# Low parts on VectorE, grouped activations and a start in program order, in a one-core mLSTM and retention block

## The chip, the cores and the metric

One core of a Trainium2 chip runs the whole block for a batch of one. The metric is the device time of one execution in microseconds (us), the median of several runs. In the profile PE is TensorE (PEld its weight loads), DVE VectorE, ACT ScalarE, POOL GpSimd and SP SyncE, whose queue issues most of the loads.

## The reference

The input has 1024 positions of width 1024; 16 learned meta positions go ahead of them, so the stream has 1040. Everything is float32.

```python
def reference(x, meta_tokens, ...):
    h = concat([meta, x])
    h = h + token_mixer(rmsnorm(h, norm_mix_g), w_in, ...)
    h = h + channel_mixer(rmsnorm(h, norm_ffn_g), ...)
    return rmsnorm(h, norm_final_g)[:, N_META:]

def token_mixer(u, ...):
    proj = u @ w_in                     # q, k, v, o, i, f of 4 mLSTM heads; q, k, v, g of 4 retention heads
    q, k = silu(causal_dwconv(ml_q, ml_k))
    li = 15 * tanh(i / 15); lf = log_sigmoid(f)
    h_ml = sigmoid(ml_o) * head_norm(mlstm_chunkwise(q, k, v, li, lf))
    h_rt = silu(rt_g) * head_norm(retention_chunkwise(rotary(rt_q), rotary(rt_k), rt_v, log_gamma))
    return concat([h_ml, h_rt]) @ w_out

def channel_mixer(u, w_up, w_gate, ffn_conv_w, w_down):
    return (silu(causal_dwconv(u @ w_up)) * (u @ w_gate)) @ w_down
```

The mLSTM weights its scores with exponentials of the gates; the gates need running sums and maxima along the sequence. Inner width of the channel mixer is 2816.

## The kernel before

**Products.** Every large product is made of three matmuls in fp32r: each float32 operand is split into a high part (a cast, on ACT) and a low part (value less high part, a subtraction), and hi·hi, hi·lo and lo·hi are summed in PSUM. In the names, `hi_` and `lo_` are the parts of a weight tile, `raw_` is the tile as loaded, and `u11h`, `u11l` are the parts of the normed stream.

**Stages.** The stream lies in quarters: 11 and 12 are the lower and upper half of the width for the first half of the positions, 21 and 22 those of the second half. Projections to q, k and o go through a scheme with seven products in place of eight (`wino_fm`, `ROWS`); it needs four sums of quarters, S1 to S4, each with a high and a low part. `usum` forms the sums on DVE, and `usplit` splits them: the high part on ACT, the low part on DVE for S1 and S2 and on POOL (`G`) for S3 and S4. The order of the seven products is 11, 12, S2, S1, S3, S4, 22. Their results leave PSUM in `wino_fm`'s evacuations (L826 to L832): copies on ACT (L828, L830) and sums on DVE (L832).

**The first norm** is cut into five ranges of positions, r = 0 to 4. `norm_sums` squares a range (ACT, or half of it on DVE for r < 2), folds the squares on DVE (not for r = 1, which takes eight column sums on PE in place of two), lets PE form column sums (tile `pca`, L688) and takes the root and reciprocal (L690, L691). `norm_split` broadcasts the result on PE (tile `pra`, L700), scales the stream on DVE (L739), casts the high part on ACT (L740) and subtracts for the low part (L744). Between the ranges stand the products for which the range that is ready suffices: `v4_group` (v of head 4 and all gate columns, one chunk of 128 positions, tile `pv`, L800) and `q4_group` (q and k of head 4, tile `pq`, L750 to L752). Then come o, q and k of the heads in the seven-product scheme (tiles `po4x`, `pq0x`, `pq0y`).

**What sets the order.** Each engine runs its instructions in one fixed order. A list scheduler of the framework, which simulates a timeline, makes these orders when the kernel is built: an instruction that is ready by its estimate can go ahead of one that was written earlier. `watch` is called for each instruction as it is written. While `pinned[0]` is true it adds a dependency, without a semaphore, of each PE, DVE and ACT instruction on the one written before it on the same engine; here `pinned[0]` is never true. Once `dealt[0]` is true, side tasks (generators) are advanced between matmul groups by `tick` and `one`, according to a running estimate of each engine's load. `rush` makes them run to their end at once.

**Side tasks that use ACT's function tables**: `sig_tasks` (sigmoid of o for the mLSTM, silu of g for retention, tile `sig`, L871, one task for each half of the width), `tables_tasks` (the mLSTM's decay table `A`: two reads from a scratch in HBM, L955 and L956, a mask, L967 and L968, then nine exponentials with a bias from `cols`, L974), the silu of q and k, the root in the head norm (`z`), and `gates` (tanh, exp, ln, with scans on DVE, tiles `gates`, `gsm`). Between activations of different functions ACT has to load a table (ACT_TABLE_LOAD).

Two copies on POOL (tile `x12`, L1618) and the low parts of S3 and S4 (L1598) are all that POOL does of size in the first 110 us.

Of the kernel before, what the change touches and what calls it, by code (L numbers as in the profile page):

```python
# [65 lines left out]
def body(ctx, tc, h_in, vecs, cst, mask_in, rot, w_v0, w_vp, w_g, w_out, w_up, w_gate, w_down, out):  # L66
# [245 lines left out]
    rush = [False]  # L312

# [37 lines left out]
    def parts(key, pairs, src):  # L351
        for i, (hi, lo) in enumerate(pairs):
            m = AC.copy(hi, src[:, i * HB:(i + 1) * HB])
            if not dealt[0]:
                after(m, last["first"])
# [18 lines left out]
    def need(key, ahead=None):  # L374
# [14 lines left out]
        if mixing[0] and key not in done:  # L389
# [320 lines left out]
    norms = {}  # L710

    def norm_sums(r):
        half, j0, j1 = RNG[r]
        n = j1 - j0
        xs = [xf[f"{half + 1}{i + 1}"][:, :, j0:j1] for i in (0, 1)]
        sq = [x[:, :, j0:j1] for x in sqs]
        AC.activation(sq[0], xs[0], AF.Square)
        if r < 2:
            m = V.tensor_tensor(sq[1], xs[1], xs[1], ALU.mult)
            if r:  # L720
                after(m, last["scale"])
        else:
            AC.activation(sq[1], xs[1], AF.Square)
        if r == 1:
            ss = [x[:, k] for x in sq for k in range(4)]
        else:
            V.tensor_tensor(sq[0], sq[0], sq[1], ALU.add)
            V.tensor_tensor(sq[0][:, 0:2], sq[0][:, 0:2], sq[0][:, 2:4], ALU.add)
            ss = [sq[0][:, k] for k in range(2)]
        norms[r] = xs, rms_sums(ss[0], 0, n, f"a{r}", tmp.tile([P, 5], F32, tag="rcol", name=f"rcola{r}"), "tr", ss[1:])  # L730

    def norm_split(r):
        half, j0, j1 = RNG[r]
        xs, got = norms.pop(r)
        pr = rms_rows(got, None, "upd")
        parts_ = [[u[:, :, j0:j1] for u in UB[f"{half + 1}{i + 1}"]] for i in range(2)]
        for i, x in enumerate(xs):
            for k in range(4):
                last["scale"] = V.scalar_tensor_tensor(x[:, k], x[:, k], vec[:, V_MIX + 4 * i + k:V_MIX + 4 * i + k + 1], pr, ALU.mult, ALU.mult)  # L739
            m = AC.copy(parts_[i][0], x)  # L740
            if r == 0:
                last["first"] = m
        for x, (h_, l_) in zip(xs, parts_):
            last["pace"] = V.tensor_tensor(l_, x, h_.bitcast(F32), ALU.subtract)  # L744
        if r == 0:
            for i, x in enumerate(xs):
                V.tensor_copy(ug[:, 4 * i:4 * i + 4], x[:, :, :32])
# [17 lines left out]
    def v0_split():  # L765
        for i in range(2):
            AC.copy(w0hi[i], w0raw[i])
            G.tensor_tensor(w0lo[i], w0raw[i], w0hi[i].bitcast(F32), ALU.subtract)

# [9 lines left out]
    def v4_group(c, tag, between=None):  # L779
        t0, L = CH[c]  # L780
        nv = 264
        pv = pp(f"pv4_{c}", tag)
        if c == 0:
            for i in range(2):
                for j in range(4):
                    PE.matmul(pv[32 * j:32 * j + 32, :nv], ug[:, 4 * i + j, :], w0raw[i][:, j * nv:(j + 1) * nv],
                                     start=i == 0, stop=i == 1, tile_position=(0, 32 * j))
            t = vz[:META, 264:264 + nv]
            spawn(quads(t, pv, nv))
            V.tensor_copy(gts[:META, :, 0, :], t[:, DV:].rearrange("p (a b) -> p a b", a=2))  # L790
            return
        half = c > 4
        j0 = t0 - 512 * half
        for i, j in ((0, 0), (0, 1), (1, 0)):
# [1525 lines left out]
```

## Time and profile before

| | |
|---|---|
| median of 3 runs | 1550.17 us (1550.03 to 1552.51) |
| the profiled execution | 1552.23 us |
| its span, first to last instruction | 1550.4 us |
| mean granted TensorE clock | 0.987 |
| busy: PE, DVE, ACT, POOL | 97%, 70%, 50%, 5% |

A line of a timeline has the start and the duration in us, engine, line of the program, operation, output and inputs by the program's names, the tile's size, and how many instructions of a kind follow one another; in brackets stands the idle time ahead of it and what ended it. A line of the windows has the stretch, its length, busy time and count for PE, PEld, DVE, ACT and POOL, then the granted clock (1.00 is full speed), the share of time in which the DMA engines were busy, and GB/s; asked for PE alone, it has PE's busy time only. A line of the waits names the waiting instruction, what it waited for, the total in us, the count and the mean. Durations of DVE or ACT groups marked xN cover N instructions.

### The profile page before, as it was taken

How to read it: one execution, taken by the hardware profiler on the slowest of the kernel's cores; microseconds unless marked ns; L12 is line 12 of the kernel's file. 1: busy time of each engine (PE TensorE's matmuls, PEld its weight loads, DVE VectorE, ACT ScalarE, POOL GpSimd, SP SyncE). 2: the span in 40 equal slices, each digit the busy share in tenths (PEclk: the TensorE clock that was granted, in tenths of full speed). 3: DMA queues.
4: the chain of work that ended last, by engine and by line, in shares of the span. 5: the costliest groups of instructions: out<-in, count | busy, mean ns of one | idle time of the engine just before them, and what ended most of it. 6: DMA issues, size and time to landing. Idle time of an engine off the chain costs nothing.

```text
span 1550.4 us, 25495 instructions
## 1 busy us (share of the span) xinstructions
PE 1503.9 (97%) x9929; PEld 1361.5 (88%) x9929; DVE 1080.2 (70%) x2103; ACT 772.2 (50%) x1467; POOL 83.8 (5%) x137
## 2 busy tenths in 40 slices
PE   7988999999999999999999999999999999999997
PEld 6978998899889999997888988999999999888887
DVE  7695867676677567755768778667666666778657
ACT  5365647574665345644355455444444444434443
POOL 1030000000000000000000001222220000000000
PEclk8999999999999999999999999999999999999999
DMA  6021345333632355589333327887873223933213
GB/s 228 1 82 56 109 132 179 99 98 122 206 95 90 109 170 177 188 308 334 121 106 119 103 80 229 209 211 190 196 190 89 82 82 121 385 113 108 100 45 109
DMA packets 104586, 223.81 MB, mean 144 GB/s; under 512 B 10520, under 2 KB 33760, under 8 KB 104288
## 3 DMA queue, kind: packets, MB, share of 16 engines
q1 hardware_dynamic: 95872, 199.02, 38.6%
q0 software_dynamic: 8448, 23.07, 7.5%
q8 instruction: 78, 1.28, 0.3%
q14 instruction: 44, 0.36, 0.1%
q10 hardware_dynamic: 144, 0.07, 0.0%
HBM read 178.05 MB, written 67.15 MB: 158 GB/s over the span
## 4 chain that ended last, share of the span: by engine, by line
PE 85%; DMA 7%; DVE 4%; ACT 3%; issue 1%; SPq 0%; DVEq 0%; ACTq 0%
PE pdx L762 3%; PE pdx L761 3%; PE pdx L760 3%; PE pup_x L761 2%; PE pup_x L762 2%; PE pup_x L760 2%; PE pga_x L760 2%; PE pga_x L761 2%; PE pga_x L762 2%; PE pdy L762 2%; PE pdy L761 2%; PE pdy L760 2%; PE pv L800 2%; PE pwx L762 2%; PE pwx L760 2%; PE pwx L761 2%
## 5 line engine op out<-in xcount | busy, mean ns | idle before, releaser
L644 ACT CAST hi_up<-raw_up 128x512 fp32r<-128x512 f32 (+1 forms) x52 | 36.4, 719 | 107.3 <-PE pga_z L761 61.1
L760 PE MATMUL pup_x<-uh_g,hi_up 128*128 128x256 f32 (+1 forms) x240 | 67.4, 283 | 1.2 <-ACT uh_g L1731 1.2
L645 DVE TENSOR_TENSOR lo_ga<-fraw_ga,hi_ga 128x512 fp32r<-128x512 f32 (+1 forms) x52 | 41.8, 807 | 37.3 <-ACT hi_ga L644 37.1
L645 DVE TENSOR_TENSOR lo_up<-raw_up,hi_up 128x512 fp32r<-128x512 f32 (+1 forms) x52 | 41.3, 809 | 37.9 <-ACT hi_up L644 37.0
L761 PE MATMUL pup_x<-ul_g,hi_up 128*128 128x256 f32 (+1 forms) x240 | 67.5, 283 | 0.1
L762 PE MATMUL pup_x<-uh_g,lo_up 128*128 128x256 f32 (+1 forms) x240 | 66.5, 283 | 0.0
L645 DVE TENSOR_TENSOR lo_d<-rd,hi_d 128x1024 fp32r<-128x1024 f32 (+1 forms) x34 | 37.6, 1112 | 32.8 <-ACT hi_d L644 32.7
L644 ACT CAST hi_ga<-fraw_ga 128x512 fp32r<-128x512 f32 (+1 forms) x52 | 36.4, 719 | 45.1 <-PE pup_z L761 24.0
L762 PE MATMUL pdx<-uh_d,lo_d 128*128 128x512 f32 (+1 forms) x156 | 57.9, 375 | 0.0
L761 PE MATMUL pdx<-ul_d,hi_d 128*128 128x512 f32 (+1 forms) x156 | 57.8, 374 | 0.0
L644 ACT CAST hi_d<-rd 128x1024 fp32r<-128x1024 f32 (+1 forms) x34 | 32.3, 959 | 49.3 <-PE pdy L761 32.5
L762 PE MATMUL pdy<-uh_d,lo_d 128*128 128x512 f32 x132 | 51.9, 393 | 0.0
L761 PE MATMUL pdy<-ul_d,hi_d 128*128 128x512 f32 x132 | 51.7, 392 | 0.0
L760 PE MATMUL pdx<-uh_d,hi_d 128*128 128x512 f32 (+1 forms) x156 | 48.5, 372 | 0.0
L760 PE MATMUL pdy<-uh_d,hi_d 128*128 128x512 f32 x132 | 47.9, 389 | 0.0
L760 PE MATMUL pga_x<-uh_g,hi_ga 128*128 128x512 f32 x120 | 47.5, 396 | 0.0
L761 PE MATMUL pga_x<-ul_g,hi_ga 128*128 128x512 f32 x120 | 47.5, 396 | 0.0
L760 PEld LDWEIGHTS pup_x<-uh_g,hi_up 128*128 128x128 f32 x240 | 45.4, 190 | 2.3 <-ACT uh_g L1731 1.4
L762 PE MATMUL pga_x<-uh_g,lo_ga 128*128 128x512 f32 x120 | 47.1, 393 | 0.0
L761 PEld LDWEIGHTS pup_x<-ul_g,hi_up 128*128 128x128 f32 x240 | 45.5, 190 | 1.0 <-DVE ul_g L1732 0.3
L762 PEld LDWEIGHTS pup_x<-uh_g,lo_up 128*128 128x128 f32 x240 | 44.8, 189 | 0.8
L526 POOL DMA_DIRECT2D wsd<-w_down_d x33 | 19.9, 748 | 467.1 <-DVE s2up L1959 466.6
(1685 smaller groups left out, 5814.4 us busy)
## 6 DMA issues: line engine op xcount, KB each, us to landing
raw_up<-w_up_d SPq DMA_DIRECT2D x22, 512.0 KB, 4.3
fraw_ga<-w_gate_d SPq DMA_DIRECT2D x22, 512.0 KB, 4.2
acts<-cv SPq DMA_DIRECT2D x44, 256.0 KB, 4.3
wsd<-w_down_d POOLq DMA_DIRECT2D x44, 256.0 KB, 6.6
rd<-wsd SPq DMA_DIRECT2D x22, 512.0 KB, 3.6
raw_w<-w_out_d SPq DMA_DIRECT2D x20, 512.0 KB, 4.2
wsw<-raw_w SPq DMA_DIRECT2D x32, 256.0 KB, 3.2
raw_m<-w_out_d SPq DMA_DIRECT2D x14, 512.0 KB, 4.9
```

Of the source, the lines that this page charges most:

```text
L526: dep(G.dma_start(x, y), last["pace"], True)
L644: AC.copy(hi[:, o:o + n], x)
L645: V.tensor_tensor(lo[:, o:o + n], x, hi[:, o:o + n].bitcast(F32), ALU.subtract)
L760: m.append(PE.matmul(pt, ah, xh_, start=first and k == 0, stop=False, skip_group_check=True))
L761: PE.matmul(pt, ah, xl_, start=False, stop=False, skip_group_check=True)
L762: m.append(PE.matmul(pt, al, xh_, start=False, stop=last and k == n - 1, skip_group_check=True))
L800: PE.matmul(pv[:, :nv], u[:, kb % 4, j0:j0 + L], (w0hi, w0lo)[j][kb // 4][:, o:o + nv], start=i + j + kb == 0, stop=i == 1 and kb == KB - ...
```

## The change

The edit has three parts.

1. The low parts of S3 and S4 are subtracted on DVE (`V`), as those of S1 and S2 are.
2. Side tasks that use a function table take turns. `table_turn(who)` lets a task go on when no other one holds the turn; `table_free()` gives it back. Both halves of `sig` are now one task, and so are the nine exponentials of `A`. `gates` doesn't ask for the turn.
3. The start is written out as one sequence, with `pinned[0]` true from the first square to the low part of range 4. Groups of matmuls are cut finer (`v4` takes one of the three products and some of the contraction blocks), `q4_group` runs its three products one after another rather than side by side, all five ranges fold their squares, and range 1 squares on ACT alone. The cast of the second half of head 4's v weights (`w0hi[1]`) is written after the root of range 0. The splits of q's weights are held in `hold` and ended at a chosen place. Chunks 5 to 8 and the rest stand behind the pinned part.

```diff
@@ -283,10 +283,15 @@
     evacs = []
     dealt = [False]
 
+    hold = []
+
     def spawn(g, q=pend):
         if dealt[0]:
             if next(g, pend) is not pend:
                 q.append(g)
+        elif hold:
+            next(g)
+            hold.append(g)
         else:
             for _ in g:
                 pass
@@ -310,6 +315,16 @@
                     q.remove(g)
 
     rush = [False]
+    turn = [None]
+
+    def table_turn(who):
+        while dealt[0] and not rush[0] and turn[0] not in (None, who):
+            yield
+        turn[0] = who
...
+    def table_free():
+        turn[0] = None
...
@@ -351,7 +366,7 @@
     def parts(key, pairs, src):
         for i, (hi, lo) in enumerate(pairs):
             m = AC.copy(hi, src[:, i * HB:(i + 1) * HB])
-            if not dealt[0]:
+            if not dealt[0] and not pinned[0]:
                 after(m, last["first"])
         yield
         for i, (hi, lo) in enumerate(pairs):
...
         issue(i + 1 + ahead)
-        if mixing[0] and key not in done:
+        if mixing[0] and not hold and key not in done:
             forced.append(key)
             rush[0] = True
             while key not in done:
...
-
-    def norm_sums(r):
+    def xr(r, i):
...
+    def square(r, i, vector=False):
+        if vector:
+            V.tensor_tensor(sqr(r, i), xr(r, i), xr(r, i), ALU.mult)
...
-    def norm_split(r):
+            AC.activation(sqr(r, i), xr(r, i), AF.Square)
+
+    def fold(r):
+        a, b = sqr(r, 0), sqr(r, 1)
+        V.tensor_tensor(a, a, b, ALU.add)
+        V.tensor_tensor(a[:, 0:2], a[:, 0:2], a[:, 2:4], ALU.add)
+
+    def sums_(r):
+        a = sqr(r, 0)
+        return rms_sums(a[:, 0], 0, a.shape[2], f"a{r}", tmp.tile([P, 5], F32, tag="rcol", name=f"rcola{r}"), "tr", [a[:, 1]])
...
+    def ur(r, i, j):
         half, j0, j1 = RNG[r]
...
+        return UB[f"{half + 1}{i + 1}"][j][:, :, j0:j1]
+
+    def scale(r, i, pr):
+        x = xr(r, i)
+        for k in range(4):
+            V.scalar_tensor_tensor(x[:, k], x[:, k], vec[:, V_MIX + 4 * i + k:V_MIX + 4 * i + k + 1], pr, ALU.mult, ALU.mult)
+        last["first"] = AC.copy(ur(r, i, 0), x)
+
+    def low(r, i):
+        last["pace"] = V.tensor_tensor(ur(r, i, 1), xr(r, i), ur(r, i, 0).bitcast(F32), ALU.subtract)
 
...
-    def v4_group(c, tag, between=None):
...
+
+    def v4_first():
+        nv = 264
...
+        yield
+        yield from quads(t, pv, nv)
...
+        yield
+
+    def v4(c, i, j, kbs=range(KB)):
...
+        if c not in bank4:
+            bank4[c] = pp(f"pv4_{c}", next(ring0))
...
+        for kb in kbs:
...
+            PE.matmul(bank4[c][:, :nv], u[:, kb % 4, j0:j0 + L], (w0hi, w0lo)[j][kb // 4][:, o:o + nv], start=i + j + kb == 0, stop=i == 1 and kb == KB - 1, skip_group_check=True)
+
+    def v4_out(c):
+        pv = bank4[c]
+        AC.copy(vtile[4][c > 4][:, (c - 1) % 4 * VW:(c - 1) % 4 * VW + DV], pv[:, :DV])
...
+
+    def q4_group(i, half, j0, j1):
+        w = ready["q4", i]
+        pt = pp(f"pq4{i}{half}{j0}", next(ring0))[:, :j1 - j0]
+        for n, (a, b) in enumerate(((0, 0), (1, 0), (0, 1))):
             for kb in range(KB):
...
-    def q4_group(i, half, j0, j1, tag):
...
+                PE.matmul(pt, w[kb // 4][b][:, kb % 4 * P:(kb % 4 + 1) * P], UB[f"{half + 1}{kb // 4 + 1}"][a][:, kb % 4, j0:j1], start=n + kb == 0, stop=n == 2 and kb == KB - 1, skip_group_check=True)
+            yield
         AC.copy(raws[i][:, half * 512 + j0:half * 512 + j1], pt)
+        yield
...
@@ -866,11 +881,16 @@
...
     def sig_tasks(h):
-        def f(b):
+        def f():
             yield from lag(1.5)
-            AC.activation(sigt[:, b], sigt[:, b], AF.Sigmoid if h < H else AF.Silu)
-            done.add(("sig", h, b))
-        return [(lambda b=b: f(b), 0, None) for b in range(2)]
+            yield from table_turn(("sig", h))
+            for b in range(2):
+                AC.activation(sigt[:, b], sigt[:, b], AF.Sigmoid if h < H else AF.Silu)
+                done.add(("sig", h, b))
+                if b == 0:
+                    yield
+            table_free()
+        return [(f, 0, None)]
 
...
@@ -967,11 +987,15 @@
...
+            yield
+            yield from table_turn(("tab", h))
             for x in (range(5), range(5, NCH)):
-                yield
...
                     AC.activation(A1[:, t0:t0 + L], A1[:, t0:t0 + L], AF.Exp, bias=cols[:, 0, c * H + h:c * H + h + 1])
+                if x[0] == 0:
+                    yield
+            table_free()
             done.add(("tab", h))
         return [(make, 0, None)]
 
@@ -1002,9 +1026,11 @@
...
+            yield from table_turn(("qk", h))
             for i in range(2):
                 d = qk[i][1]
                 AC.activation(d[:, a:b], d[:, a:b], AF.Silu)
+            table_free()
             done.add(("qk", h, r))
 
...
@@ -1436,9 +1462,12 @@
...
                 yield
+                yield from table_turn(("z", h))
                 AC.activation(z[:, :n], z[:, :n], AF.Sqrt)
             else:
+                yield from table_turn(("z", h))
                 AC.activation(z[:, :n], mv[:, 0:n, 1], AF.Sqrt, bias=cs[:, C_EPS + h - H:C_EPS + h - H + 1])
+            table_free()
             yield
...
@@ -1557,26 +1586,102 @@
...
-    norm_sums(0)
-    v0_split()
-    norm_split(0)
-    v4_group(1, next(ring0), lambda: norm_sums(1))
-    need(("q4", 0), 1)
-    norm_split(1)
-    v4_group(0, next(ring0))
-    v4_group(2, next(ring0))
-    norm_sums(2)
-    q4_group(0, 0, 0, 272, next(ring0))
-    norm_split(2)
-    q4_group(1, 0, 0, 272, next(ring0))
-    norm_sums(3)
-    for c in (3, 4):
-        v4_group(c, next(ring0))
-    norm_split(3)
-    norm_sums(4)
+    def end(g):
+        for _ in g:
+            pass
+
+    def v4_all(c):
+        for i, j in ((0, 0), (0, 1), (1, 0)):
+            v4(c, i, j)
+
+    lower, upper = range(4), range(4, KB)
+    pinned[0] = True
+    square(0, 0)
+    square(0, 1, True)
+    fold(0)
+    AC.copy(w0hi[0], w0raw[0])
+    pr = rms_rows(sums_(0), None, "upd")
     for i in range(2):
-        q4_group(i, 0, 272, SB, next(ring0))
-    norm_split(4)
+        if i:
+            AC.copy(w0hi[i], w0raw[i])
+        G.tensor_tensor(w0lo[i], w0raw[i], w0hi[i].bitcast(F32), ALU.subtract)
+    square(1, 0)
+    scale(0, 0, pr)
+    square(1, 1)
+    scale(0, 1, pr)
+    v4(1, 0, 0)
+    fold(1)
+    v4(1, 0, 1, lower)
+    got = sums_(1)
+    low(0, 0)
+    v4(1, 0, 1, upper)
+    v4(1, 1, 0, lower)
+    low(0, 1)
+    v4(1, 1, 0, upper)
+    pr = rms_rows(got, None, "upd")
+    hold.append(None)
+    need(("q4", 0), 0)
+    for i in range(2):
+        V.tensor_copy(ug[:, 4 * i:4 * i + 4], xr(0, i)[:, :, :32])
+    scale(1, 0, pr)
+    v4_out(1)
+    scale(1, 1, pr)
+    meta = v4_first()
+    next(meta)
+    need(("q4", 1), 0)
+    v4(2, 0, 0)
+    v4(2, 0, 1)
+    low(1, 0)
+    low(1, 1)
+    v4(2, 1, 0)
+    end(hold[1])
+    square(2, 0)
+    square(2, 1)
+    fold(2)
+    end(hold[2])
+    hold.clear()
+    end(meta)
+    q = q4_group(0, 0, 0, 272)
+    next(q)
+    next(q)
+    got = sums_(2)
+    v4_out(2)
+    next(q)
+    pr = rms_rows(got, None, "upd")
+    scale(2, 0, pr)
+    end(q)
+    scale(2, 1, pr)
+    q = q4_group(1, 0, 0, 272)
+    for _ in range(3):
+        next(q)
+    square(3, 0)
+    square(3, 1)
+    end(q)
+    low(2, 0)
+    low(2, 1)
+    fold(3)
+    v4_all(3)
+    v4_out(3)
+    got = sums_(3)
+    v4_all(4)
+    pr = rms_rows(got, None, "upd")
+    scale(3, 0, pr)
+    scale(3, 1, pr)
+    v4_out(4)
+    square(4, 0)
+    square(4, 1)
+    end(q4_group(0, 0, 272, SB))
+    low(3, 0)
+    low(3, 1)
+    fold(4)
+    got = sums_(4)
+    end(q4_group(1, 0, 272, SB))
+    pr = rms_rows(got, None, "upd")
+    scale(4, 0, pr)
+    scale(4, 1, pr)
+    low(4, 0)
+    low(4, 1)
+    pinned[0] = False
...
@@ -1595,7 +1700,7 @@
...
             AC.copy(h_, part(x, i))
-            (G if nm in ("S3", "S4") else V).tensor_tensor(l_, part(x, i), h_.bitcast(F32), ALU.subtract)
+            V.tensor_tensor(l_, part(x, i), h_.bitcast(F32), ALU.subtract)
 
...
@@ -1605,13 +1710,15 @@
...
     for c in (5, 6):
-        v4_group(c, next(ring0))
+        v4_all(c)
+        v4_out(c)
     for i in range(2):
-        q4_group(i, 1, 16, 272, next(ring0))
+        end(q4_group(i, 1, 16, 272))
     for c in (7, 8):
-        v4_group(c, next(ring0))
+        v4_all(c)
+        v4_out(c)
     for i in range(2):
-        q4_group(i, 1, 272, SB, next(ring0))
+        end(q4_group(i, 1, 272, SB))
     usplit("S3", "21", "r2", "r3")
```

Three places of the new order, each before and after.

PE around the column sums of the last range (`pca_529` before, `pca_551` now). Before:

```order
L700 MATMUL pra_508<-cs,rcola_444 128x16
L700 MATMUL pra_508<-cs,rcola_444 128x128 x2
L688 MATMUL pca_529<-cs,sqr_132 128x1 x4
L750 MATMUL pq_536<-u11h,hi_q_0_0_289 128x256
L751 MATMUL pq_536<-u11l,hi_q_0_0_289 128x256
```

Now, from the q products (`pq_681`) that stand ahead of them:

```order
L822 MATMUL pq_681<-u22h,hi_q_0_0_283 128x256
L822 MATMUL pq_681<-u21l,hi_q_0_0_283 128x256 x4
L822 MATMUL pq_681<-u22l,hi_q_0_0_283 128x256 x4
L703 MATMUL pca_551<-cs,sqr_132 128x1 x4
L822 MATMUL pq_558<-u11h,hi_q_1_0_310 128x256 x4
```

The sums moved from behind the broadcast of range 3 to behind chunks 5 and 6 and most of a q group of the second half of the positions, none of which is in the pinned part.

ACT from the last copy of head 4's gate to head 0's first q evacuation (`rawq<-pq0x`). Before:

```order
L828 COPY sig<-po4x_895 128x256
L353 CAST hi_q_3_0_1180<-raw_q0b 128x512
L353 CAST hi_q_3_0_1180<-raw_q0a 128x512
L871 ACT_TABLE_LOAD
L871 ACTIVATE sig<-sig 128x1026 x2
L353 CAST hi_q_5_0_1283<-raw_q0b 128x512
L353 CAST hi_q_5_0_1283<-raw_q0a 128x512
L1109 ACT_TABLE_LOAD
```

Now:

```order
L843 COPY sig<-po4x_891 128x256
L888 ACT_TABLE_LOAD
L888 ACTIVATE sig<-sig 128x1026
L1120 ACT_TABLE_LOAD
L1120 ACTIVATE gsm<-gsm 1x36
L1042 COPY rawq<-rawk 64x528
L1043 COPY rawq<-rawk 64x528
L368 CAST hi_q_3_0_1176<-raw_q0b 128x512
L368 CAST hi_q_3_0_1176<-raw_q0a 128x512
L1042 COPY rawq<-rawk 64x512
L1043 COPY rawq<-rawk 64x512
L888 ACT_TABLE_LOAD
```

The two halves of the gate's silu were neighbours with one load; now the exponential of the gates (`gsm`), four copies of the rotary and two casts stand between them: the exponential has a load of its own, and the second half has to load its table again.

ACT at head 0's decay table (`A_0`). Before:

```order
L830 ACTIVATE rawk<-pq0x_1234 128x264
L353 CAST hi_vp_0_0_1431<-raw_vp_11_1308 128x512 x2
L830 ACTIVATE rawk<-pq0x_1257 128x264
L974 ACTIVATE A_0_1642<-A_0_1642,cols 128x16
L974 ACTIVATE A_0_1642<-A_0_1642,cols 128x128 x2
```

Now:

```order
L845 ACTIVATE rawk<-pq0x_1230 128x264
L995 ACTIVATE A_0_1638<-A_0_1638,cols 128x16
L995 ACTIVATE A_0_1638<-A_0_1638,cols 128x128 x8
L368 CAST hi_vp_0_0_1437<-raw_vp_11_1304 128x512 x2
L845 ACTIVATE rawk<-pq0x_1253 128x264
```

All nine exponentials and the two casts moved ahead of the second evacuation of `pq0x`. In the whole order there are 46 table loads now, 44 before.

More of the change, by code (lines that the diff above doesn't have):

```diff
@@ L732, in norm_split @@
-    def norm_split(r):
-        half, j0, j1 = RNG[r]
[L734 to L747, printed above, removed]
+        return xf[f"{half + 1}{i + 1}"][:, :, j0:j1]
@@ L763, in mm3s @@
         return m[0], m[-1]
[L765 to L768, printed above, removed]
     def quads(dst, pv, n):
@@ new lines, in body @@
+    square(1, 0)
[14 more added lines that the diff above has]
+    need(("q4", 0), 0)
+    for i in range(2):
+        V.tensor_copy(ug[:, 4 * i:4 * i + 4], xr(0, i)[:, :, :32])
[3 more added lines that the diff above has]
+    meta = v4_first()
```

52 lines of the change are left out of this document (12 added, 40 removed).

## The prediction

> **What bounds the kernel now.** I read the page first, then the PE windows, then the timelines of the first 135 us, because the order of instructions differs only in short stretches.
>
> ```profile
> PE 1503.9 (97%) x9929; PEld 1361.5 (88%) x9929; DVE 1080.2 (70%) x2103; ACT 772.2 (50%) x1467; POOL 83.8 (5%) x137
> PE 85%; DMA 7%; DVE 4%; ACT 3%; issue 1%; SPq 0%; DVEq 0%; ACTq 0%
> 0.00:80.00 80.00, 69.19 (x487) 66.91 (x488) 56.64 (x111) 37.63 (x60) 8.12 (x10) 0.94 0.32 111
> 80.00:120.00 40.00, 30.51 (x229) 28.27 (x227) 34.74 (x69) 24.25 (x42) 11.63 (x5) 0.91 0.25 80
> 120.00:600.00 480.00, 469.47 (x3622) 439.93 (x3623) 327.62 (x774) 270.03 (x547) 8.46 (x44) 0.99 0.41 127
> ```
>
> TensorE (PE) is the bound; its idle time is 46.5 us of the span, 20.3 us of it before 120 us (10.8 and 9.5). So a gain can only come from there, or from a clock that is granted earlier. How fast PE runs depends on that clock:
>
> ```profile
> 34.04 1.08 PE L800 MATMUL pv<-w0hiq,u11l 128*128 128x264 f32 x4
> 34.92 1.08 PE L800 MATMUL pv<-w0hik,u12l 128*128 128x264 f32 x4
> 41.74 0.65 PE L800 MATMUL pv<-w0hiq,u11h 128*128 128x264 f32 x4
> 42.23 0.65 PE L800 MATMUL pv<-w0hik,u12h 128*128 128x264 f32 x4
> 34.00:36.00 2.00, 2.00 (x11) 0.50 0.00 0
> 100.00:102.00 2.00, 0.25 (x2) 0.75 0.61 173
> 106.00:108.00 2.00, 2.00 (x12) 0.55 0.00 0
> ```
>
> Four matmuls take 0.88 us at a clock of 0.50 and 0.49 us at 1.00, so 0.22 and 0.122 each (0.126 for 272 columns and 0.1185 for 256, by the same spacing). The dip at 101 us lasts about 6.8 us and costs half of that; it begins at the end of a PE wait.
>
> **The start, to the last matmul of the norm stage.** In the new order the square root of the first norm goes ahead of the cast of w0hik, and the second norm adds its squares on VectorE (DVE), so its column sums are 2 float32 matmuls and not 8.
>
> ```profile
> 8.87 1.07 ACT L767 CAST w0hik<-w0raw 128x1056 fp32r<-128x1056 f32 x1 [0.28 <-DMA w0raw<-w_v_d]
> 9.85 0.26 ACT L690 ACTIVATE rcola<-pca,vec 128x2 f32<-128x2 f32 x1
> 11.37 1.71 PE L688 MATMUL pca<-cs,sqr 128*128 128x1 f32 x8
> 13.56 1.25 PE L800 MATMUL pv<-w0hiq,u11h 128*128 128x264 f32 x4 [0.49 <-ACT u11h L740]
> ```
>
> The first large matmul moves from 13.56 to 12.7 (0.85 for the cast). Six float32 matmuls at two records of 0.22 each are 2.7 us less. Followed through with the durations above, pv of chunk 2 ends at 28.4; before, it ended at 35.6 (34.92 and four matmuls). That is 7.2 us, but not all of it is kept. Before, PE had by then done column sums of ranges 2 and 3 as well; now these are still ahead. From 28.4 there are 48 matmuls of 0.126 (6.05), 144 of 0.122 (17.6), 144 of 0.1185 (17.1), 4.9 of norm matmuls and 0.4 at half clock: 46.0. To this come waits which program order makes, because range 3's norm follows range 2's with little between: 1.05 for u12h, 1.4 for the folded squares, 1.2 for u22h. Sum 28.4 + 46.0 + 3.7 = 78.1, against 78.3 before. I take nothing for the start. Bounds: 2.5 better, if the clock rises one stretch earlier (24 matmuls at 0.122), 2 worse, if a wait lets it fall.
>
> **The last norm comes late.** At the first place shown in the section on the change, the column sums of range 4 (pca) followed the broadcast of range 3 (pra) at once. The sums now stand behind chunks 5 and 6 and most of a q group, which are not pinned and were hoisted.
>
> ```profile
> 55.43 3.22 DVE L739 SCALAR_TENSOR_TENSOR x<-x,vec,pra 128x256 f32<-128x256 f32 x8 [1.16 <-PE pra L700]
> 71.50 1.25 DVE L1598 TENSOR_TENSOR uS2l<-x,uS2h 128x1056 fp32r<-128x1056 f32 x1
> 91.87 0.38 PE L760 MATMUL po4x<-uS2h,hi_o 128*128 128x256 f32 x1 [2.49 <-ACT sig L828]
> ```
>
> DVE's scaling starts at 63.1 instead of 55.43 (PE reaches the sums at 58.7, then 24 matmuls, then the broadcast). Behind it DVE has 25.6 us without a pause up to the low part of S2, which ends at 88.7 and not at 72.7. PE needs it at 86.7: new waits of about 2.0, then 2.3 for S1's high part and the evacuations. They replace waits of 3.5 us (2.49, 0.78, 0.22) there. Price so far +0.8.
>
> **Low parts of S3 and S4 on DVE.** What GpSimd (POOL) does to DVE:
>
> ```profile
> 80.38 5.77 POOL L1598 TENSOR_TENSOR uS3l<-x,uS3h 128x1056 fp32r<-128x1056 f32 x2
> 81.23 5.47 DVE L358 TENSOR_TENSOR lo_o<-raw_o4b,hi_o 128x512 fp32r<-128x512 f32 x2 [0.27 <-ACT hi_o L353]
> 101.95 1.28 DVE L358 TENSOR_TENSOR lo_q<-raw_q0a,hi_q 128x512 fp32r<-128x512 f32 x2
> 95.28 5.48 POOL L1598 TENSOR_TENSOR uS4l<-s,uS4h 128x1056 fp32r<-128x1056 f32 x2 [9.13 <-ACT uS4h L1597]
> 94.98 0.38 DVE L1071 TENSOR_TENSOR_SCAN gates<-gates 36x128 f32<-36x128 f32 x1
> 98.42 2.62 DVE L1073 TENSOR_TENSOR_SCAN gates<-gates 36x128 f32<-36x128 f32 x1
> PE pe L1079 <- DVE gsm L1075: 3.0, 1, 3.0
> ```
>
> Beside POOL, two DVE splits took 5.47 instead of 1.28 and a scan 2.62 instead of 0.38; with one more gate step that is 8.6 us. The four moved parts add 4 x 1.17 = 4.7 (L1598 at 1.25, less overlap). DVE is 3.9 us ahead, the scan is no longer held, PE's 3.0 us wait goes and the dip at 101 us with it. The two copies on POOL (L1618) stay. Carried through, PE ends the matmuls of po4x with u22 at 104.7 instead of 109.7: 5.0 ahead.
>
> **Grouped activations give it back.** Counted in the two orders, table loads rise from 44 to 46. At the second place shown, ACT between the last copy of o4 and q0's first evacuation, one half of head 4's output gate (tile sig) went ahead of the gates' exponential (gsm), so the other half, further down, needs a load of its own.
>
> ```profile
> L871 ACT ACT_TABLE_LOAD x11 | 14.1, 1283 | 0.2
> 109.95 0.35 ACT L828 COPY sig<-po4x 128x256 f32<-128x256 f32 x1
> 112.89 2.01 ACT L871 ACTIVATE sig<-sig 128x1026 f32<-128x1026 f32 x2
> 119.96 0.63 ACT L828 COPY rawq<-pq0x 128x264 f32<-128x264 f32 x2
> 120.37 0.39 PE L760 MATMUL pq0x<-uS2h,hi_q 128*128 128x264 f32 x1 [3.38 <-ACT rawq L828]
> ```
>
> From the copy at 104.9, ACT has three loads before the last one, four in all (5.1), the two halves of sig (2.0), four rotary copies (2.5, L1042 and L1043, which ran earlier before), four casts (2.1), the gates' small steps and copies (1.8): 13.5, so 118.4 against 120.37. PE, which arrives at 112.4, waits 6.0 instead of 3.4 us. Of 5.0 ahead 2.0 are left.
>
> Next, the third place, head 0's table A. The evacuation of pq0x's second chunk, for which PE waits before S3, now stands behind all nine exponentials and two casts, and those wait for a transfer through HBM.
>
> ```profile
> 0.00:24.00 24.00, 15.02 (x74) 12.83 (x74) 12.78 (x33) 13.34 (x21) 5.18 (x8) 1.00 0.98 341
> ...
> 120.49 0.35 SPq L955 DMA_DIRECT2D A<-scr  x1
> 121.37 2.27 SPq L956 DMA_DIRECT2D A<-scr  x2
> 124.33 0.18 DVE L967 TENSOR_TENSOR A<-A,mask 128x16 f32<-128x16 f32 x1 [3.21 <-DMA A<-scr]
> 126.49 0.38 ACT L830 ACTIVATE rawk<-pq0x 128x264 f32<-128x264 f32 x1
> 127.54 1.22 DVE L968 TENSOR_TENSOR A<-A,mask 128x1024 f32<-128x1024 f32 x1 [3.03 <-DMA A<-scr]
> 130.09 1.85 ACT L974 ACTIVATE A<-A,cols 128x128 f32<-128x128 f32 x6
> 131.95 0.29 PE L760 MATMUL pq0y<-uS4h,hi_q 128*128 128x264 f32 x1
> 135.73 0.49 PE L1353 MATMUL s<-qT,kT 128*128 128x128 f32 x2 [0.97 <-DVE pt L1377]
> ```
>
> The read of A is issued at about 119.6 (1.8 earlier), with two weight tiles (raw_vp, 512 KB each) ahead of it in place of one. Before, from the first issue at 121.37 the second piece took some 6 us to the mask add at 127.54; one more weight tile takes 1.5 at the 341 GB/s of the window of the first 24 us (DMA busy share 0.98); so it lands near 127.2; mask 1.2, cols 0.2, nine exponentials 2.6, two casts 1.1, the evacuation 0.3: PE goes on at 132.6. Before, it started that group at 130.5 (131.95 less 12 matmuls). So 2.1 late; PE is there at 128.7 and waits 3.9. The later wait of 0.97 for DVE is covered now, which makes +1.1.
>
> A wait of this length ends in a dip. The dips of the trace cost 3.4 (6.8 us) and 1.7 (that at 121 us); the one at 121 us has its counterpart after the wait of 6.0, the second wait adds one. I take the mean, 2.5. All the rest I cost at nothing: the second extra load lies near 315 us under PE at 100%, and if ACT has no slack there it costs 1.3; from about 665 us on the orders agree.
>
> The Trainium skill (TensorE: Matmul & The Clock Gate, section "Why this matters for your kernels") states that gaps above about 3 us between bursts take the clock down. The trace agrees for the wait of 3.0 ahead of 101 us. By the page's busy window of about 3.4 us a dip would cost an estimated 1.7, and the sum would be 0.8 lower.
>
> **Sum.** 0 (start) + 0.8 - 5.8 = -5.0 at 104.7; +3.0 on ACT; +4.1 at A's exponentials; -1.0; +2.5 clock: **+3.6 us**. The profiled execution has a span of 1550.4 and took 1552.23, so it would be 1555.8; the median of the runs, 1550.17, lies 2.06 below that execution, which gives **1553.8**.
>
> **Rivals.** *The exponentials don't hold PE* (faster). If A lands in 3.8 us, as its first piece did (issued 120.49, used 124.33), ACT is through by 128.8 and PE hardly waits: -2.0, -1.0, and no second dip; from a landing before 123.5 on this decides. 1547. For it: the transfer itself is small; against: two weight tiles are ahead.
>
> *The hold without the dip* (no change): +1.1, 1551.3. A wait of 2.49 at 89 us left the clock at 1.00; against it: 3.0 and 3.4 did not.
>
> *Dips everywhere* (slower): the broken stretch at 86 to 92 us and a wait in the start each cost a dip too: +3.6 + 2 x 2, 1558. For it: PE is busy there about a third of the time; against: from 87 to 92 it was hardly busier before, at 1.00.
>
> **How the numbers follow.** Forecast 0.42, faster rival 0.22, no change 0.20, dips 0.16. A measurement of this kernel tells about 0.2%, 3.1 us, from no change; the forecast lies just above it, and I split it 0.27 slower, 0.13 no change, 0.02 faster. The faster rival lies at the bound too: 0.19 faster, 0.03 no change. Of the no-change case 0.13 stay there, 0.06 are slower, 0.01 faster. With the dips that makes faster 0.22, no change 0.29, slower 0.49. Range 1546 to 1561: downward the faster rival with another 1 of the start's 2.5; upward the dips with the start's 2 and the 1.3 at 315 us. The forecast's own range is 1551.5 to 1556.5.
>
> **What would show it.** Right: scaling of range 4 starts near 63; PE waits near 88 for uS2l, near 112 to 118 for rawq, and some 4 us at S3 of q0 for rawk behind the exponentials; the clock at 0.50 after both; no DVE split above 2 us but beside POOL's copies. Wrong: PE without a wait from 125 to 135, or ahead by 3 us or more at 140, or behind already at 78.

## The result and the profile after

The changed kernel takes 1564.04 us (median of 4 runs, 1560.94 to 1566.96), the kernel before beside it 1551.32. The ratio is 1.0084, 95% interval [1.0067, 1.0102]: slower by 12.7 us, where 3.6 were forecast. The profiled execution took 1564.91 us with a span of 1562.2, 11.8 more than before.

The page of the changed kernel (busy time of each engine) and its windows, with the columns of those before:

```profile
PE 1503.5 (96%) x9917; PEld 1359.8 (87%) x9917; DVE 1079.2 (69%) x2108; ACT 774.3 (50%) x1470; POOL 75.0 (5%) x133
0.00:80.00 80.00, 62.33 (x447) 58.63 (x448) 46.56 (x101) 29.78 (x51) 5.19 (x8) 0.94 0.37 124
80.00:120.00 40.00, 34.03 (x257) 31.86 (x256) 36.83 (x73) 28.59 (x46) 3.56 (x2) 0.96 0.18 54
120.00:600.00 480.00, 461.01 (x3519) 431.31 (x3520) 321.67 (x762) 266.69 (x535) 10.66 (x44) 0.98 0.39 123
```

PE's busy time is the same to 0.4 us (1503.9 before). So the whole 11.8 us are idle time of PE: 6.9 more before 80 us (17.7 against 10.8), 3.5 less from 80 to 120 (6.0 against 9.5), 8.5 more from 120 to 600 (19.0 against 10.5).

The waits in the start, from PE's timeline:

```profile
12.66 1.25 PE L810 MATMUL pv<-w0hiq,u11h 128*128 128x264 f32 x4 [1.99 <-ACT u11h L755]
21.28 0.76 PE L810 MATMUL pv<-w0hiq,u11h 128*128 128x264 f32 x4 [0.83 <-ACT u11h L755]
23.43 1.25 PE L810 MATMUL pv<-w0hik,u12h 128*128 128x264 f32 x4 [1.39 <-ACT u12h L755]
36.92 0.75 PE L810 MATMUL pv<-w0hiq,u11h 128*128 128x264 f32 x4 [1.90 <-ACT u11h L755]
42.68 1.81 PE L703 MATMUL pca<-cs,sqr 128*128 128x1 f32 x12 [1.49 <-DVE gts L815]
55.52 0.75 PE L810 MATMUL pv<-w0hik,u22h 128*128 128x264 f32 x4 [0.88 <-ACT u22h L755]
```

At ranges 0 to 3 PE waits for the cast that follows the scaling; the row at 42.68 is the exception, column sums that wait for DVE, where a copy of the gates stands behind the folded squares. The last matmul of the stage ends at 83.6 us; it was 78.4 before. DVE behind it:

```profile
67.23 3.22 DVE L754 SCALAR_TENSOR_TENSOR x<-x,vec,pra 128x256 f32<-128x256 f32 x8 [2.92 <-PE pra L715]
86.70 1.24 DVE L1703 TENSOR_TENSOR uS2l<-x,uS2h 128x1056 fp32r<-128x1056 f32 x1
89.68 2.41 DVE L1703 TENSOR_TENSOR uS3l<-x,uS3h 128x1056 fp32r<-128x1056 f32 x2
92.02 1.24 DVE L1703 TENSOR_TENSOR uS2l<-x,uS2h 128x1056 fp32r<-128x1056 f32 x1
96.42 2.34 DVE L1703 TENSOR_TENSOR uS1l<-s,uS1h 128x1056 fp32r<-128x1056 f32 x2
```

Range 4 is scaled from 67.2 (55.43 before), and from there DVE has no pause up to 99 us. It was idle 2.9 us just ahead, waiting for PE. The second half of S2's low part is through at 93.3 (72.7 before), and for it PE waits 1.0 us. ACT, PE and DVE at the gates:

```profile
111.69 0.37 ACT L843 COPY sig<-po4x 128x256 f32<-128x256 f32 x1 [2.23 <-PE po4x L773]
112.08 1.28 ACT L888 ACT_TABLE_LOAD   x1
113.37 1.06 ACT L888 ACTIVATE sig<-sig 128x1026 f32<-128x1026 f32 x1
114.45 1.28 ACT L1120 ACT_TABLE_LOAD   x1
119.74 1.28 ACT L888 ACT_TABLE_LOAD   x1
123.14 1.28 ACT L1135 ACT_TABLE_LOAD   x1
125.23 0.66 ACT L843 COPY rawq<-pq0x 128x264 f32<-128x264 f32 x2
135.88 2.64 ACT L995 ACTIVATE A<-A,cols 128x16 f32<-128x16 f32 x9 [6.50 <-DVE cols L1143]
...
125.62 0.40 PE L1142 MATMUL pt<-cs,gates 36*128 36x36 f32 x2 [5.82 <-DVE gates L1138]
135.90 0.61 PE L1379 MATMUL s<-qT,kT 128*128 128x16 f32 x2 [3.08 <-DVE cols L1143]
...
130.37 0.18 DVE L987 TENSOR_TENSOR A<-A,mask 128x16 f32<-128x16 f32 x1 [3.62 <-DMA A<-scr]
133.13 1.22 DVE L446 TENSOR_TENSOR raw_vp<-raw_vp,raw_vp 128x1024 f32<-128x1024 f32 x1 [2.58 <-DMA raw_vp<-w_vp_d]
134.44 1.22 DVE L988 TENSOR_TENSOR A<-A,mask 128x1024 f32<-128x1024 f32 x1
135.58 0.26 DVE L1143 COPY cols<-pt 128x108 f32<-128x108 f32 x1
```

Four loads between 112 and 124.4, and PE waits 5.8 us until it can transpose the gates, which come out of these exponentials. Another wait of 3.1 us follows at 133 to 136: PE's score matmul `s` needs the copied columns (`cols`), and on DVE these stand behind a sum of weights (`raw_vp`), which waits 2.6 us for its load, and behind the second part of the mask of `A`.

### The profile page after: what moved, and what is told of

It reads as the page before. It is cut to its first block, busy times and chain, and to the rows that moved or that the text cites. A ratio compares the mean times of both kernels' runs of the same rounds, so it can differ in the third digit from the quotient of the medians.

```text
span 1562.2 us, 25485 instructions
## 1 busy us (share of the span) xinstructions
PE 1503.5 (96%) x9917; PEld 1359.8 (87%) x9917; DVE 1079.2 (69%) x2108; ACT 774.3 (50%) x1470; POOL 75.0 (5%) x133
## 4 chain that ended last, share of the span: by engine, by line
PE 83%; DVE 7%; DMA 6%; ACT 3%; issue 1%; SPq 0%; DVEq 0%; ACTq 0%
PE pdx L773 3%; PE pdx L772 3%; PE pdx L771 3%; PE pup_x L772 2%; PE pup_x L773 2%; PE pga_x L771 2%; PE pup_x L771 2%; PE pga_x L772 2%; PE pga_x L773 2%; PE pdy L773 2%; PE pdy L772 2%; PE pdy L771 2%; PE pwx L773 2%; PE pwx L771 2%; PE pwx L772 2%; PE n L1429 2%
## 5 line engine op out<-in xcount | busy, mean ns | idle before, releaser
L772 PE MATMUL pdx<-ul_d,hi_d 128*128 128x512 f32 (+1 forms) x156 | 57.8, 374 | 0.0
L659 ACT CAST hi_d<-rd 128x1024 fp32r<-128x1024 f32 (+1 forms) x34 | 32.3, 959 | 48.8 <-PE pdy L772 32.5
```

Of the source, the lines that this page charges most:

```text
L659: AC.copy(hi[:, o:o + n], x)
L772: PE.matmul(pt, ah, xl_, start=False, stop=False, skip_group_check=True)
```

## The experiments

All times are medians beside runs of the kernel before on the same chip; the ratio is to those. Chips differ by a microsecond or two, so kernels of different sets are compared by their ratios (0.001 is 1.55 us). An idle time or a place in a timeline is that of the one execution that was profiled, which lies up to 5 us from its kernel's median.

**The three parts apart.** Each kernel has one or two of them. Undoing or doing a part is, for the low parts and the turns:

```diff
-            (G if nm in ("S3", "S4") else V).tensor_tensor(l_, part(x, i), h_.bitcast(F32), ALU.subtract)
+            V.tensor_tensor(l_, part(x, i), h_.bitcast(F32), ALU.subtract)
```

```diff
+            yield from table_turn(("sig", h))
...
+            table_free()
```

together with the one task for both halves in `sig_tasks` and for all exponentials in `tables_tasks`. The start is that of one kernel or the other.

Low parts alone.

> The kernel before with one edit: the low parts of S3 and S4 on DVE. Theory A (my prediction's second step): without POOL beside it DVE is no longer held up, PE's wait of 3.0 us at 98 us and the half-clock stretch behind it go, so the last product of head 4's gate ends about 5 us earlier (104 in place of 109.2) and the whole is 3 to 5 us faster, near 1547. Rival: DVE is 4.7 us busier just where PE waits for it, so the gain is eaten at once and the time stays within 2 us of 1551.

Turns alone.

> The kernel before with one edit: side tasks that use a function table take turns. Theory A: the turns cost PE waits by themselves, at head 0's q (3 to 7 us before its S3 products) and at head 2's q (3.5 us near 300 to 345 us): 1556 to 1561. Rival B (the start alone is to blame, and whatever follows is only late with it): within 2 us of 1551.

Start alone.

> The changed kernel with the other two edits undone, so that of the change only the start in program order is left. Theory A: 5.2 us late at the first product of head 4's gate (83.5 in place of 78.2), and little after it: 1554 to 1557. Rival B: the same 5.2 us there, and most of the later loss with it: 1560 to 1564.

Low parts and turns with the old start.

> The kernel before with the low parts on DVE and the turns, but its own start. Theory A: 5 us gained at head 4's gate and 5 to 8 lost behind it: 1551 to 1556. Rival B: 1546 to 1550, the low parts' gain and no loss.

The change without the turns.

> The changed kernel without the turns; the start in program order and the low parts on DVE stay. Theory A: PE's waits for the gates (5.8 us at 120 us) and for the copied columns behind A (3.1 us at 133 us), and those near 290 to 345 us, shrink by 4 us together: 1558 to 1561. Rival (the waits come from the late start alone): 1563 to 1565.

The change with the low parts back on POOL.

> The changed kernel with the low parts of S3 and S4 back on POOL. If they are worth nothing at the end: 1562 to 1566, as the changed kernel. If a busier DVE is what hurts behind a late norm: 3 us or more faster; if DVE beside POOL is slower still: 3 us or more slower.

| parts in the kernel | us | ratio [95%] |
|---|---|---|
| low parts | 1549.88 | 0.9995 [0.9981, 1.0009] |
| turns | 1552.71 | 1.0013 [0.9995, 1.0031] |
| low parts, turns | 1554.74 | 1.0030 [1.0014, 1.0045] |
| start | 1560.49 | 1.0060 [1.0039, 1.0082] |
| start, low parts | 1561.16 | 1.0061 [1.0040, 1.0082] |
| start, turns | 1562.35 | 1.0073 [1.0045, 1.0101] |
| all three | 1564.04 | 1.0084 [1.0067, 1.0102] |

By the ratios of the pairs of rows that differ in one part, the start costs 8.4 to 10.2 us, the turns 2.0 to 5.4, the low parts between -0.8 and +2.6; the intervals of the rows are 2 to 4 us to either side, so only the start's cost is certain in each pair. The rival "the start alone is to blame" is nearer than my theory, which had put most of the loss on the turns. With the low parts alone the gain that I had forecast is there at 120 us and gone at 200: in the windows of PE (second figure of a row: busy time), idle from 80 to 165 us falls from 10.8 to 2.7, and 9.5 us come back at 165 to 200, where head 4's norm holds PE. Before, low parts alone:

```profile
80.00:165.00 85.00, 74.17 (x538) 0.94 0.25 75
```

```profile
80.00:165.00 85.00, 82.29 (x642) 1.00 0.30 94
...
PE tr L1458 <- ACT v4lo L1449: 4.7, 1, 4.7
PE tr L1458 <- DVE mx L1466: 2.3, 1, 2.3
```

The last two rows are PE's waits from 165 to 200 us. PE had run ahead with products of the next head and then had nothing to put beside head 4's chain.

In the kernel with start and low parts but without the turns, ACT has the same order behind the start, four loads between the same activations, and PE the same wait of 5.8 us for the gates; its wait for `cols` is 1.7 us there and not 3.1. So most of what I had called the turns' doing isn't theirs. What is theirs lies later: the wait for `rawk` and for the merge (`mx`) near 320 to 340 us is there with them and not without, first the changed kernel from 285 to 350 us, then the one without turns:

```profile
PE tr L1487 <- DVE mx L1495: 1.6, 1, 1.6
PE pq2x L771 <- DVE rawk L847: 1.6, 2, 1.2
```

```profile
PE s L1358 <- DVE pt L1377: 0.8, 1, 0.8
```

**What in the start costs it.** First without program order, the flag staying false:

```diff
-    pinned[0] = True
+    pinned[0] = False
```

> The changed kernel with the start's instructions free again (the flag stays false there), its code as it is. Theory S1 (program order itself makes PE wait): PE's idle time in the first 60 us falls from 17.7 to about 11 us, head 4's gate begins near 78 in place of 83.5, and the whole comes to that of the two other edits alone, 1553 to 1557. Theory S2 (what was rewritten in the start makes the waits: folded squares of range 1, q's three products one after another, held splits): idle stays at 16 us or more, 1561 to 1566.

Measured 1556.20, ratio 1.0039 [1.0022, 1.0056]. That is 7.0 us below the changed kernel, though PE's idle time in the first 60 us is 15.2, between the numbers of the two theories: from 80 to 165 us 2.1 us are idle and not 14.7, and at 165 to 200 us 9.8 come back, as with the low parts alone. So the order costs some 7 us, and the waits in the start, 2.5 us shorter, are not where most of them go.

Then program order on DVE and ACT only:

```diff
-        if pinned[0] and nm in before:
+        if pinned[0] and nm != "PE" and nm in before:
```

> The changed kernel with only PE free of the program order in the start; DVE and ACT keep it. If PE's own order makes the waits (products that are ready stand behind ones that are not): idle of the first 60 us falls to 11 to 13 us, 1553 to 1558. If it is the order on DVE and ACT (the norms come late, whatever PE does meanwhile): idle stays at 16 us or more, 1561 to 1566.

1562.71, ratio 1.0083 [1.0053, 1.0113]: nothing gained, and 16.6 us are idle in the first 60. It is DVE's and ACT's order.

Program order kept longer, up to head 4's last q group:

```diff
     low(4, 1)
-    pinned[0] = False
...
     for i in range(2):
         end(q4_group(i, 1, 272, SB))
+    pinned[0] = False
```

> The changed kernel with program order kept up to the last q group of head 4, so that chunks 5 and 6 can't go ahead of the column sums of range 4. Theory L (the late sums cost time at S2 of head 4's gate): DVE scales range 4 from about 60 and not from 67, PE's 1.0 us wait for the low part of S2 and part of the waits by it go, 1559 to 1562. Rival: chunks 5 and 6 filled holes that open again, so nothing is gained: 1563 to 1567.

1577.05, ratio 1.0173 [1.0147, 1.0200]. A miss on both sides, and it doesn't test what it was made for: DVE's gate copies now stand in order behind the sums and splits of S1 and S2, the PSUM banks stay taken, and PE waits 7.2 us for one of these copies alone; range 4 is scaled at 67.8, no earlier.

**The norms earlier, still in program order.** Squares, folds, sums and broadcasts of ranges 2 to 4 one range ahead:

```diff
     fold(1)
+    square(2, 0)
+    square(2, 1)
...
+    fold(2)
+    square(3, 0)
...
-    square(2, 0)
-    square(2, 1)
-    fold(2)
+    fold(3)
+    scale(2, 0, pr)
...
+    square(4, 0)
+    square(4, 1)
```

> The changed kernel, still in program order, with the norm's steps written earlier: squares, folds, column sums and broadcasts of ranges 2, 3 and 4 stand one range ahead. Theory N (program order costs time because it was written with each range's norm just ahead of its use, so that PE, ACT and DVE wait for one another in turn): PE's idle time in the first 60 us falls from 17.7 to 11 to 13 us, head 4's gate begins at 75 to 79 in place of 83.5, and head 0's q, reached earlier, loses the waits of 5.8 and 3.1 us: 1550 to 1556. Rival (any order fixed by hand loses against the scheduler's): idle stays at 15 us or more and the time at 1558 or above.

1551.57, ratio 1.0009 [0.9997, 1.0022]: 11.6 us below the changed kernel. The time agrees with theory N, its reason doesn't: idle in the first 60 us is 20.1 and head 4's gate begins at 86.1, later than in the changed kernel. What is gained lies behind:

```profile
0.00:80.00 80.00, 59.93 (x408) 0.87 0.33 111
80.00:165.00 85.00, 83.86 (x661) 1.00 0.26 80
57.78 3.22 DVE L754 SCALAR_TENSOR_TENSOR x<-x,vec,pra 128x256 f32<-128x256 f32 x8
79.80 1.24 DVE L1703 TENSOR_TENSOR uS1l<-s,uS1h 128x1056 fp32r<-128x1056 f32 x1
```

Range 4 is scaled at 57.8 and S1 is split at 79.8, ahead of PE; from 80 to 165 us PE is idle 1.1 us. Then without the turns, and with the low parts on POOL too:

> As the last, without the turns. Theory N with the turns costing some 3 us by themselves: 1547 to 1553, at or below the kernel before. If the turns cost nothing with an early start: the same as the last within 2 us.

> As the last, with the low parts of S3 and S4 back on POOL as well: of the change only program order in the start is left, with the norm's steps earlier. If the low parts on DVE are worth nothing at the end, as they were alone: the same as the last within 2 us. If they help once the start is early: 2 to 4 us slower than the last.

1548.30, ratio 0.9982 [0.9971, 0.9993], and 1553.66, ratio 1.0022 [1.0011, 1.0033]. The turns cost 3.3 us; and here the low parts on DVE are worth 5.4, more than the 2 to 4 expected.

**Only the last range.** In the changed kernel, range 4's steps one group earlier:

```diff
     got = sums_(3)
-    v4_all(4)
+    square(4, 0)
+    square(4, 1)
+    v4(4, 0, 0)
+    v4(4, 0, 1)
     pr = rms_rows(got, None, "upd")
+    fold(4)
+    got = sums_(4)
+    v4(4, 1, 0)
...
-    square(4, 0)
-    square(4, 1)
     end(q4_group(0, 0, 272, SB))
-    low(3, 0)
-    low(3, 1)
-    fold(4)
-    got = sums_(4)
-    end(q4_group(1, 0, 272, SB))
     pr = rms_rows(got, None, "upd")
     scale(4, 0, pr)
     scale(4, 1, pr)
+    end(q4_group(1, 0, 272, SB))
+    low(3, 0)
+    low(3, 1)
```

> The changed kernel with one edit: squares, fold, column sums and scaling of range 4 are written one group earlier, so that its column sums stand ahead of chunk 5. Theory R4 (the late last norm puts DVE 12 us behind and so makes the waits from 80 to 165 us): DVE scales range 4 near 57 in place of 67, PE's idle time in the first 60 us stays at 16 to 18, that from 80 to 165 us falls from 14.7 to below 5, and the whole is 1550 to 1556. Rival (all ranges must come earlier): 1558 to 1564.

1553.05, ratio 1.0016 [0.9998, 1.0035]: 10.5 us gained by one move, which also puts the low parts of range 3 behind range 4's scaling. From its DVE timeline, its windows and its ACT timeline:

```profile
61.29 3.22 DVE L754 SCALAR_TENSOR_TENSOR x<-x,vec,pra 128x256 f32<-128x256 f32 x8 [2.77 <-PE pra L715]
86.82 2.43 DVE L1705 TENSOR_TENSOR uS1l<-s,uS1h 128x1056 fp32r<-128x1056 f32 x2 [1.25 <-ACT uS1h L1704]
...
80.00:165.00 85.00, 82.00 (x639) 0.98 0.26 75
...
110.37 2.01 ACT L888 ACTIVATE sig<-sig 128x1026 f32<-128x1026 f32 x2
```

The changed kernel's row for the same stretch:

```profile
80.00:165.00 85.00, 70.33 (x500) 0.92 0.18 51
```

Idle from 80 to 165 us falls from 14.7 to 3.0, though range 4 is scaled at 61.3 and not near 57, as expected. And the scheduler, which places everything behind the start by its own estimate of when DVE is free, leaves the two halves of `sig` together.

The converse, range 4's place left late in the kernel with early norms; then, without the turns, the kernel with range 4 one group earlier; then the converse without the turns:

> The run with the norms written earlier, but range 4's norm as late as in the changed kernel. Theory R4: the waits from 80 to 165 us come back, DVE scales range 4 near 66, 1557 to 1564. Rival: within 2 us of 1551.6, as the run with all norms early.

> As the first of this set, without the turns. If the turns cost some 3 us as in the pair with all norms early: 3 us below the first of this set. If they cost nothing: within 1 us of it.

> The run with all norms early but range 4's in its late place, without the turns. By the pairs so far the turns cost 3 us: 1545 to 1548, faster than the kernel before by 0.15 to 0.35%. If the turns cost nothing here: 1549.

The first: 1549.37, ratio 0.9989 [0.9975, 1.0003], so the rival holds as far as the order goes. But the place in the order isn't the time: with ranges 2 and 3 early PE is idle only 11.9 us in the first 60 us, comes to range 4 sooner and DVE scales it at 57.8 all the same. It doesn't show that a late range 4 is harmless. It shows something else: PE's idle time up to 165 us is 21.7 us here, 21.2 in the kernel with all norms early and 21.6 in the kernel before, and those three lie within about 3 us of each other; the changed kernel has 32.3. Waits of 8 us went from the start to the stage behind it and the time stayed. The second: 1550.38, ratio 0.9993 [0.9974, 1.0013], 2.7 us less than with the turns. The third: **1544.26, ratio 0.9965 [0.9950, 0.9979]**, the fastest of all, 5.4 us below the kernel before and 18 below the changed one. It has program order in the start and the low parts on DVE, with the norms of ranges 2 and 3 early and no turns.

**ACT's order behind the start.** The changed kernel with two rules more:

```diff
+        last["gx"] = AC.activation(b, b, AF.Exp, scale=2.0)
...
+                if h == 4:
+                    after(m, last["gx"])
...
+                    if h == 0:
+                        after(m, last["rk"])
```

> The changed kernel with its start as it is, and two rules for ACT behind it: both halves of head 4's sig after the gates' exponentials, and head 0's exponentials of A after the second negative copy of q0. Theory O (ACT's order makes the waits): the gates' last exponential comes 5 to 6 us sooner, PE's wait of 5.8 us for it falls below 2 and idle from 120 to 145 us from 8.7 below 4: 1556 to 1559. Rival (PE waits there since DVE is late by the last norm, whatever ACT does): within 2 us of 1564.

1559.80, ratio 1.0061 [1.0037, 1.0085]; its interval overlaps that of the changed kernel, so the 3.6 us between the ratios are not sharp. The trace shows them in place: idle from 120 to 145 us 1.7 and not 8.7, the wait for `cols` gone, that for the gates 4.3 us, where less than 2 was expected, and it ends at 121.6 and not at 125.6. Of these 4.0 us, 2.1 were there when head 4's gate began (81.4 against 83.5), with the same start.

```profile
80.00:165.00 85.00, 75.21 (x537) 0.94 0.20 59
...
121.58 0.40 PE L1150 MATMUL pt<-cs,gates 36*128 36x36 f32 x2 [4.27 <-DVE gates L1146]
```

So ACT's order makes perhaps 3.6 of the 10.5 us that hang on the late last norm. The rest I put down to DVE itself; that is by difference, and no run of its own shows it.

Over all 19 kernels the time at which DVE scales range 4 parts them in two: where it does so at 61.3 us or earlier, the ratios are 0.9965 to 1.0039, where at 65.1 or later, 1.0060 to 1.0173. Within each group the times don't follow it.

## Why the prediction went wrong, step by step

How far behind the kernel before each of the two executions stands at five places, in us, as forecast and as found in the profiles:

| place | forecast | found | this stage, forecast | this stage, found |
|---|---|---|---|---|
| first matmul of head 4's gate | 0 | +5.3 | 0 | +5.3 |
| end of its last product (22) | -5.0 | +2.4 | -5.0 | -2.8 |
| first S2 product of head 0's q | -2.0 | +5.6 | +3.0 | +3.1 |
| first S3 product there | +2.1 | +10.0 | +4.1 | +4.4 |
| head 0's o begins (197 us) | +3.6 | +8.9 | +1.5 | -1.1 |
| end | +3.6 | +11.8 | 0 | +2.9 |

- **The start, taken at nothing**, is the term that failed most: 5.3 us late in this pair of profiles, and 8.4 to 10.2 us at the end by the kernels that differ in it. Up to the end of chunk 2 the count was good (27.5 against 28.4; the end before, by the row that the prediction names, is 35.8 and not 35.6, which the sum doesn't use). From there to head 4's gate 56.0 us were found, where 49.7 had been added up. Of the 6.3 us between, some 3.0 are clock: it was 0.50 for 6.8 us from 43.6 on, which costs 3.4, where the sum had 0.4, and "2 worse, if a wait lets it fall" stood only among the bounds. 1.5 are waits, 5.2 us in place of 3.7: the three that had been counted came to 3.2 together, and 1.9 for `u11h` of range 2 hadn't been. 1.1 are 16 matmuls into `pvm`, which now go ahead of the gate; the remaining 0.7 I can't place. Before, the squares of ranges 2 to 4 were done by 25.9 us, which the same trace shows; now range 4's are done at 57.7, and each range's norm goes from PE to ACT, DVE, PE, DVE and ACT just ahead of its use.

  Four matmuls at half clock and those into `pvm`, from PE's timelines, after and then before:

```profile
46.26 1.08 PE L810 MATMUL pv<-w0lo,u11h 128*128 128x264 f32 x4
70.89 1.07 PE L599 MATMUL pvm<-raw_vm,ug 128*32 128x256 f32 x16
```

```profile
45.62 0.65 PE L800 MATMUL pv<-w0lo,u11h 128*128 128x264 f32 x4
82.80 1.07 PE L584 MATMUL pvm<-raw_vm,ug 128*32 128x256 f32 x16
```

- **The last norm late**: place and direction right (63 was forecast, 67.2 found; the difference is the start's, since PE reached the column sums at 62.9 and not at 58.7), price wrong. I took +0.8 for it and let the low parts win 5.8 against it; the stage won 2.8, of which 1.1 are `pvm`, no longer in it. This one step, undone alone, gives back 10.5 us. The waits in the start are not the loss by themselves: the kernel with all norms early has more of them and loses nothing.
- **The low parts on DVE**: the gain to 109 us is real (alone it is 8.4 us there by the end of product 22, of which 2.5 were there at 78 us), but alone it is given back at 165 to 200 us. I hadn't followed PE beyond the stage. (POOL also forms the low parts of head 4's v weights, 2.4 us each from 8.7 and 11.0 us, which the list of its work left out; they are the same in both kernels.)
- **Grouped activations**: the sums came out (13.5 us of ACT from its last copy to q0's evacuation, 13.5 found from start to start; PE's wait 6.0, 5.8 found; behind `A` 3.9, 3.1 found), but in part by luck, since the cause was another. The order of ACT there comes with the late start; without the turns it is the same. And PE waited for the gates and not for `rawq` in the first place, for `cols` and not for `rawk` in the second.
- **"All the rest at nothing"**: behind 290 us the turns cost some 3 us, which I had bounded with 1.3. The changed kernel is 9.6 us late at head 2's q (290 us before) and 12.8 at its o (364 us before); without the turns it is 12.7 and 12.6 late there.
- **The dips**, +2.5: half-clock time up to 200 us is 23.9 us against 20.5, which is 1.7 at half speed. The stretch from 43.6 us is part of it, so that this isn't to be added to the start's loss.

The range ended 3 us too low, since its upper end took the start's loss at 2.

## What to carry to other kernels

An order fixed by hand fixes the slack too, and its price needn't be where the order is: with the norms written one range ahead PE waited longer in the start (20.1 us against 17.7), and 11.6 us were gained behind it. Count a wait by what it delays on the engine that is late next, not by its own length: here 8 us of PE's waits moved from the start to the stage behind it and the time stayed, while a last norm that came late on DVE cost 10.5. And where a scheduler places what comes behind, a late stage can be paid twice, in the delay and in the order that is chosen by it; the second part is not sharp here (3.6 us, with intervals that overlap).

## What the runs showed of the hardware

The half-clock stretch of the start isn't fixed by the instructions. Three kernels with the same start, in their profiled executions: the kernel before, low parts alone, turns alone (windows of PE; behind the busy time the granted clock):

```profile
30.00:33.00 3.00, 3.00 (x15) 0.50 0.01 3
33.00:36.00 3.00, 3.00 (x15) 0.50 0.00 0
```

```profile
30.00:33.00 3.00, 3.00 (x16) 0.50 0.00 0
33.00:36.00 3.00, 3.00 (x23) 0.88 0.00 0
```

```profile
30.00:33.00 3.00, 3.00 (x23) 0.89 0.00 0
33.00:36.00 3.00, 3.00 (x26) 1.00 0.00 0
```

It lasts 10.2, 6.8 and 3.4 us, steps of one size, and head 4's gate begins at 78.2, 75.7 and 74.3 for it. So 4 us at one place of one execution are no difference between kernels, and the forecast was reckoned from the slowest of these starts. Over all profiles, four kernels with the old start begin the gate at 74.3 to 78.2 us, five with the changed start at 81.4 to 85.9; the means are 7.7 us apart, where the pair of profiles in the table has 5.3.

The clock also fell without a wait of 3 us. In the changed kernel it was 0.50 from 43.6 us, and the waits ahead of that were 1.90, 0.81 and 1.49 us, all after 35 us; in the kernel before it fell near 26 us, in this wait of 1.83:

```profile
26.49 1.25 PE L800 MATMUL pv<-w0hiq,u11h 128*128 128x264 f32 x4 [1.83 <-ACT u11h L740]
```

How many short waits it takes, no run here shows.

A switch of ACT's table cost no more than its load. In the rows of the gates above, the load at 112.08 took 1.28 us and the next activation began at 113.37; the copy ahead of the load had ended at 112.06. The Trainium skill (ScalarE: Activation LUTs, section "What `ACT_TABLE_LOAD` costs") adds a drain of about 1380 ns, 2.66 us in all for each switch. The measurement decides: 1.31 us from activation to activation.
